# Modulation units that hold whole columns, placed later in the first mixer's load order, and the S5 matrices loaded from SyncE's queue

## The chip, the core and the metric

The kernel runs on one core of a Trainium2 chip. The metric is the device time of one execution in microseconds. All times below are of the kernel before the change.

## What is computed

The reference is two blocks over one sequence of 256 tokens, 1024 wide. Only the first part of the first block and the S5 branch of the second touch the change.

```python
def first_block(x, c, ...):
    cond = jax.nn.silu(c)
    mod = cond @ ada_w + ada_b                      # 1024 -> 6144
    sh1, sc1, g1, sh2, sc2, g2 = jnp.split(mod, 6)
    h = rms_norm(x, norm1_g) * (1.0 + sc1) + sh1
    y = hybrid_mixer(h, w_in, w_out, ...)           # four groups: attention a, attention b, GLA, LRU
    x = x + g1 * y
    h = rms_norm(x, norm2_g) * (1.0 + sc2) + sh2
    x = x + g2 * moe(h, ...)                        # 32 experts, 4 of them per token
```

The second block has two layers. Each is a SwiGLU feed-forward, a mixer (an SSD branch and an S5 branch), and a second feed-forward. The S5 branch is a diagonal complex recurrence, computed in chunks with small matrices (`win`, `E`, `toep`, `G`).

## The kernel before

Activations lie with features on the partitions, 256 tokens along the free axis. Every large weight is cut on the host into units of 128 x 2048 numbers (1 MB). `enqueue` puts all units of the program in one list. `load` issues the DMAs of this list in its order on SyncE's queue (SP), one whenever a raw buffer is free: three `raw` buffers, and two more (`rawx`) in the first mixer. A unit of a product is split into two halves, each into a high part (ScalarE, `whi`) and a low part (VectorE or GpSimd, `wlo`), and goes through TensorE in three passes (`mm3`: high by high, high by low, low by high). When both halves are split, the raw buffer is dropped and the next load is issued. A unit with a `use` function of its own is not split: `use` runs the function and drops the buffer. The 24 modulation units of `ada_w` are of this kind.

The order of work on each engine is fixed when the program is built. A planner (`Clocks`) keeps a modelled clock for each engine and for the DMA. `stir`, `tick` and `pump`, called between pieces of matrix product, step threads (attention a and b, GLA, LRU, the S5 build) when the modelled clocks say that their inputs are there. On the chip each engine then runs its own list strictly in order. Numbers such as `self.room` are counts of buffers that the planner has given out: `ps` are the eight PSUM banks, `p4` the large pages.

The first mixer (`mixer1`). The list begins with eight modulation units and two of the eleven input weights; after that come two modulation units behind each input weight, and at the end the four output weights `wo1`. Modulation unit u of `adaw` is 128 rows (one k) by 2048 columns, so eight units are needed before the first 2048 columns of `mod` are complete: `ada_unit` adds them up in one PSUM bank, which is held from unit 0 to unit 23, in four matmuls of 512 columns, each to its own 32 columns of TensorE's array. After each eighth unit `ada_turn` copies the bank to SBUF, transposes it and adds the bias. `use_up(7)` stands ahead of the products: it makes sure that shift and scale (`mod[:, :16]`) are complete. A loop over k then forms the normalised input `xn[k]`, and from k = 3 on multiplies with the first two input weights, cqk and cv, and the GLA gate. The other nine input weights follow in the order of `WIN`: cr, aq, ak, av, dx, dg, bq, bk, bv. A thread starts as soon as the products that it needs are there. Then `wo1` follows in the order of `YORD`: LRU, attention b, attention a, GLA; a group waits for its thread. The experts' weights are loaded into pages that the first mixer has used.

In the second block `ffn` consumes a unit for every 48 matmuls of 256 columns. While the first feed-forward of layer 0 and the second of layer 0 run, the thread `s5_build` loads the matrices of the next S5 branch, which were parked in DRAM during the experts: for each of two halves eight DMAs of 256 KB (`LT` from `ld`, `BT` from `s5_bt`, both read with a broadcast), a complex product of six operations (`cmul`, on GpSimd or VectorE) that makes `win`, and later four DMAs of 512 KB (`E`), sixteen of 64 KB (`toep`) and four of 512 KB (`G`). That is 40 DMAs and 9 MB in a layer. All are issued by GpSimd; the waits `GAP` between them (4 to 8 us) are of the planner's clock and place them in GpSimd's list, and are no waits on the chip.

Of the kernel before, what the change touches and what calls it, by code (L numbers as in the profile page):

```python
# [15 lines left out]
P = 128  # L16
# [179 lines left out]
class Core:  # L196
# [3 lines left out]
    stepping = GIVE = False  # L200
    KEEP = ("raw", "whi", "wlo", "ident", "causal", "ones_d", "ones_g", "eps", "one", "one32", "junk", "id16", "s5_r4", "vecs")
# [154 lines left out]
    def pump(self):  # L356

        c = self.nc
        while self.sl < self.sh and c.written(self.halves[self.sl][0]) <= max(c.tensor.clock, min(self.v.clock, self.q.clock)) + self.SOON:
            self.split_low()  # L360
        while self.sh <= min(self.most, 2 * self.last - 1) and self.arrived(self.order[self.sh // 2], c.scalar) and self.free(c.scalar):
            self.split_high()
        for u in sorted(self.uses):
            if not self.arrived(u, c.tensor):
                break
            self.use(u)
# [252 lines left out]
class Block2(Core):  # L619
# [406 lines left out]
    def s5_build(self, l, res):  # L1026
# [8 lines left out]
        for hf in range(2):  # L1035
            yield from self.need(p4=7)
            LT = self.p4([P, H, 64]), self.p4([P, H, 64])
            BT = self.p4([P, H, 64]), self.p4([P, H, 64])
            for g in range(2):
                rows = slice(g * 64, g * 64 + 64)  # L1040
                for ri in range(2):
                    self.lab = "s5b"
                    nc.gpsimd.dma_start(LT[ri][rows], dram_ap(ld, ((ri * 2 + g) * 4 * NP + hf * H) * 64, [[NP * 64, 4], [0, 16], [1, H * 64]]))
                    nc.gpsimd.dma_start(BT[ri][rows], dram_ap(a["s5_bt"], (((l * 2 + ri) * 2 + g) * 16 * NP + hf * H) * 64,
                                                            [[0, 4], [NP * 64, 16], [1, H * 64]]))
# [11 lines left out]
        for hf in range(2):  # L1057
            for ri in range(2):
                self.lab = "s5b"
                nc.gpsimd.dma_start(E[hf][ri].rearrange("p h m -> p (h m)"), made["ed"][hf, :, ri * 1024:ri * 1024 + 1024])  # L1060
# [4 lines left out]
        for hf in range(2):  # L1065
            for g in range(2):
                for j in range(4):
                    self.lab = "s5b"
                    r0 = g * 64 + j * 16
                    nc.gpsimd.dma_start(toep[hf][r0:r0 + 16], dram_ap(kd, hf * H * 32 * 112 + g * 16 * 112 + (3 - j) * 16,  # L1070
# [4 lines left out]
        for hf in range(2):  # L1075
            for ri in range(2):
                self.lab = "s5b"
                nc.gpsimd.dma_start(G[hf][ri].rearrange("p h k c -> p (h k c)"), made["gd"][hf, :, ri * 1024:ri * 1024 + 1024])
# [601 lines left out]
class Kernel(Block2):  # L1680
    NE, B1, NP42, NP22, NP12, NPAIR = 32, 2.0, 9, 8, 10, 4
    MIX = dict(EARLY=0.2, SOON=-0.5, LEAN=2.0, GIVE=True)
    WAT = 0, 3
    S3 = 0
# [7 lines left out]
    def block1_units(self):  # L1692
# [59 lines left out]
    def ada_load(self):  # L1752
# [3 lines left out]
        self.mod = self.t([P, 48], "mod")  # L1756

    def ada_unit(self, u, raw, n):

        nc = self.nc  # L1760
        g, k = divmod(u, KD)
        if not u:
            self.adaps = self.bank()
        lab, self.lab = self.lab, "ada"
        for i in range(4):
            nc.tensor.matmul(self.adaps[i * 32:i * 32 + 32], self.cond[:, k], raw[:, i * 512:i * 512 + 512], start=k == 0, stop=k == KD - 1,
                             skip_group_check=True, tile_position=(0, i * 32))
        if k == KD - 1:
            rows = self.t([P, 512], "adarow")
            nc.scalar.copy(rows, self.adaps)  # L1770
            if g == 2:
                self.give(ps=1)
            if g:
                self.defer(lambda: self.ada_turn(g, rows))
            else:
                for _ in self.ada_turn(g, rows):
                    pass
        self.lab = lab

    def ada_turn(self, g, rows):  # L1780

        nc = self.nc
        yield from self.need(ps=1)
        self.lab = "ada"
        ps = self.psum()
        for j in range(4):
            nc.tensor.transpose(ps[:, j * P:(j + 1) * P], rows[:, j * P:(j + 1) * P], self.ident)
        yield
        at = lambda t: t[:, g * 16:g * 16 + 16].rearrange("p (i j) -> p i j", j=4)
        self.v.tensor_tensor(at(self.mod), ps.rearrange("p (j i r) -> p i j r", j=4, r=32)[:, :, :, 0], at(self.vec("adab")), op=ALU.add)  # L1790
        self.give(ps=1)
# [479 lines left out]
    def mixer1(self, x):  # L2271
# [101 lines left out]
        self.use_up(self.keys.index(("ada", 23)))  # L2373
        for g in self.YORD:
# [8 lines left out]
            if last:  # L2383
                self.settle()
# [561 lines left out]
def host_block1(d, vecs, off):  # L2946
# [10 lines left out]
    out["adaw"] = c(f("ada_w").reshape(8, P, 3, 2048).transpose(2, 0, 1, 3).reshape(24, P, 2048))  # L2957
# [83 lines left out]
```

## Time and profile before

| what | us |
|---|---|
| median of three runs | 2945.7 (2922.97 to 2946.81) |
| the profiled execution, its own time | 2948.41 |
| its span, first to last instruction | 2946.7 |
| around the span | 1.7 |
| TensorE busy / DMA queue of SP, share of 16 engines | 2673.1 (91%) / 63.2% |

The span falls into stages: the first mixer to about 250 us, router and experts to about 1285, layer 0 of the second block to about 2142, and layer 1 to the end. PE is TensorE's matmuls, PEld its weight loads, DVE is VectorE, ACT is ScalarE, POOL is GpSimd; a name like `aq_raw<-adaw` is a DMA into a raw buffer from the tensor `adaw`. The prefix of a buffer's name is the label that the planner had when it was made, so modulation units have buffers of many names.

### The profile page before, as it was taken

The page shows a single profiled execution, that of the slowest core. Times are in us where ns is not written, and L with a number is a line of the kernel's source. Part 1 is how long each engine was busy: PE and PEld are TensorE (multiplying, and loading weights), DVE is VectorE, ACT ScalarE, POOL GpSimd, SP SyncE. Part 2 cuts the span into 40 slices and gives each one's busy share as a digit, 9 for nine tenths or more (in the row PEclk, how much of TensorE's full clock was granted, in tenths as well). Part 3 has the DMA queues.
Part 4 walks back from the last instruction along what each step waited for, and adds up shares of the span by engine and source line. Part 5 has one row for each costly group of instructions (what it writes and reads, how often), then busy time and mean ns, then how long its engine had stood idle before and what let it go on. Part 6 is the DMA issues. An engine that isn't in the chain of part 4 may idle for free.

```text
span 2946.7 us, 55258 instructions
## 1 busy us (share of the span) xinstructions
PE 2673.1 (91%) x22931; PEld 2049.9 (70%) x22931; DVE 1670.8 (57%) x2968; ACT 1009.0 (34%) x1474; POOL 423.4 (14%) x386
## 2 busy tenths in 40 slices
PE   6867898988898888988999999889999999998998
PEld 3656333332333333368999999889999999998998
DVE  3485324242333311056679787667575698977755
ACT  3273100001000000033454655434454455654544
POOL 2322100000000000034012131143010100221100
PEclk7788999999999999999999999999999999999999
DMA  8504999999999999977554544377455455553453
GB/s 333 214 31 146 420 420 405 415 420 420 420 415 416 420 419 419 418 243 206 203 184 167 189 172 170 137 160 241 172 189 180 149 180 189 186 190 125 159 185 115
DMA packets 145421, 754.62 MB, mean 256 GB/s; under 512 B 45760, under 2 KB 50320, under 8 KB 58640
## 3 DMA queue, kind: packets, MB, share of 16 engines
q1 hardware_dynamic: 127584, 710.42, 63.2%
q0 software_dynamic: 17440, 40.61, 5.3%
q8 instruction: 185, 3.03, 0.4%
q14 instruction: 68, 0.56, 0.1%
q10 hardware_dynamic: 144, 0.00, 0.0%
HBM read 735.98 MB, written 14.97 MB: 255 GB/s over the span
## 4 chain that ended last, share of the span: by engine, by line
PE 45%; DVE 7%; DMA 2%; ACT 2%; issue 1%; ACTq 0%; DVEq 0%
PE ffn_ps L172 21%; PE x_ps L172 4%; PE bb_ps L172 3%; PE z_ps L172 3%; PE glu_ps L172 3%; PE g_ps L172 3%; PE bnd_ps L172 2%; PE wo_ps L172 2%; DMA ffn_raw<-gu 1%; DVE ffn_wlo L172 1%; PE ssd_ps L172 1%; PE u_ps L172 1%; DVE ffn_p L172 1%; DVE x_p L172 1%; DVE bnd_p L172 1%
## 5 line engine op out<-in xcount | busy, mean ns | idle before, releaser
L172 PE MATMUL ffn_ps<-bnd_p,ffn_whi 128*128 128x256 f32 x2560 | 468.3, 285 | 0.5 <-ACT ffn_whi L172 0.5
L172 DVE TENSOR_TENSOR ffn_wlo<-ffn_raw,ffn_whi 128x1024 fp32r<-128x1024 f32 x232 | 305.5, 1322 | 189.9 <-ACT ffn_whi L172 189.8
L172 PEld LDWEIGHTS ffn_ps<-bnd_p,ffn_whi 128*128 128x128 f32 x2560 | 404.0, 194 | 0.9 <-ACT ffn_whi L172 0.9
L172 PE MATMUL ffn_ps<-bnd_p,ffn_wlo 128*128 128x256 f32 x1280 | 365.7, 286 | 17.5 <-DVE ffn_wlo L172 17.5
L172 ACT CAST ffn_whi<-ffn_raw 128x1024 fp32r<-128x1024 f32 x232 | 240.6, 1046 | 310.8 <-PE ffn_ps L172 242.1
L172 PE MATMUL down_ps<-up_place,tr_p 128*32 128x512 f32 (+1 forms) x2048 | 243.1, 612 | 81.1 <-DMA up_place<-edn 81.1
L172 PE MATMUL ffn_ps<-ffn_p,ffn_whi 128*128 128x256 f32 x1408 | 259.6, 286 | 11.3 <-ACT ffn_whi L172 11.3
L172 PEld LDWEIGHTS ffn_ps<-bnd_p,ffn_wlo 128*128 128x128 f32 x1280 | 248.5, 194 | 19.0 <-DVE ffn_wlo L172 19.0
L172 PE MATMUL up_ps<-down_place,prep_p 128*32 128x512 f32 (+1 forms) x1920 | 224.7, 596 | 21.0 <-DMA down_place<-eup 21.0
L172 PE MATMUL up_ps<-up_place,prep_p 128*32 128x512 f32 (+1 forms) x2048 | 230.5, 595 | 7.5 <-DMA up_place<-eup 7.0
L172 PEld LDWEIGHTS down_ps<-up_place,tr_p 128*32 128x32 f32 x2048 | 68.2, 112 | 243.0 <-issue 202.9
L172 PEld LDWEIGHTS ffn_ps<-ffn_p,ffn_whi 128*128 128x128 f32 x1408 | 223.3, 195 | 11.7 <-ACT ffn_whi L172 11.7
L172 DVE TENSOR_SCALAR glu_p<-up_ps 128x512 f32<-128x512 f32 x64 | 44.2, 691 | 311.2 <-PE up_ps L172 311.2
L172 PE MATMUL ffn_ps<-ffn_p,ffn_wlo 128*128 128x256 f32 x704 | 201.5, 286 | 1.1 <-DVE ffn_wlo L172 1.1
L172 PEld LDWEIGHTS up_ps<-up_place,prep_p 128*32 128x32 f32 x2048 | 61.8, 109 | 149.8 <-issue 129.8
L172 PEld LDWEIGHTS up_ps<-down_place,prep_p 128*32 128x32 f32 x1920 | 57.0, 109 | 130.7 <-issue 127.0
L172 DVE COPY scat_p<-down_ps 128x512 f32<-128x512 f32 x16 | 11.1, 692 | 240.4 <-PE down_ps L172 240.4
L172 PEld LDWEIGHTS ffn_ps<-ffn_p,ffn_wlo 128*128 128x128 f32 x704 | 137.1, 195 | 1.9 <-DVE ffn_wlo L172 1.9
L172 DVE TENSOR_TENSOR ffn_p<-ffn_p,ffn_p 128x256 f32<-128x256 f32 (+1 forms) x184 | 99.6, 547 | 41.6 <-ACT ffn_p L172 41.4
L172 ACT COPY prep_p<-prep_ps 128x512 f32<-128x512 f32 x16 | 9.4, 585 | 291.2 <-PE prep_ps L172 291.2
L172 ACT COPY tr_p<-tr_ps 128x512 f32<-128x512 f32 x32 | 18.7, 585 | 223.6 <-PE tr_ps L172 223.6
L172 PE MATMUL bb_ps<-ssd_p,ba_whi 128*128 128x256 f32 x416 | 84.2, 302 | 9.5 <-ACT ssd_p L172 6.1
(794 smaller groups left out, 5887.4 us busy)
## 6 DMA issues: line engine op xcount, KB each, us to landing
up_place<-eup SPq DMA_DIRECT2D x128, 1024.0 KB, 10.8
up_place<-edn SPq DMA_DIRECT2D x128, 1024.0 KB, 13.7
down_place<-eup SPq DMA_DIRECT2D x120, 1024.0 KB, 14.7
ffn_raw<-gu SPq DMA_DIRECT2D x75, 1024.0 KB, 4.9
ffn_raw<-dn SPq DMA_DIRECT2D x40, 1024.0 KB, 5.0
x_raw<-win SPq DMA_DIRECT2D x22, 1024.0 KB, 5.0
z_raw<-win SPq DMA_DIRECT2D x16, 1024.0 KB, 5.1
g_raw<-win SPq DMA_DIRECT2D x10, 1024.0 KB, 4.9
```

Source lines behind the costliest of these rows:

```text
L172: return f(out, *args, **kw)
```

## The change

Three things change. The modulation weights are cut by columns: unit u holds all eight k of 256 columns, so its eight matmuls complete these columns. For u below 8 they are column tile u of the shift and of the scale; for the others they are two neighbouring tiles. Each unit takes a PSUM bank of its own, and is copied, summed over the four column groups by two small matmuls with `four`, and added to its bias. At most two are under way (`room["ada"] = 2`). The loop over k asks for unit k alone, just ahead of `xn[k]`. In the list, two modulation units stand ahead of the first input weight and two ahead of the second; the other 16 follow one behind each input weight from av on (six) and behind the first two output weights (four and six). `pump` uses a modulation unit only when the modelled landing is 2.0 us ago and a bank is free, and the last ones are asked for only at the last output group. Third, all 40 DMAs of `s5_build` are issued on SP.

```diff
@@ Core.pump
         for u in sorted(self.uses):
-            if not self.arrived(u, c.tensor):
+            if u not in self.raws or c.written(self.raws[u][0]) > c.tensor.clock - self.ADAM or not self.has(dict(ps=1 + self.PSADA, ada=1)):
                 break
             self.use(u)
@@ s5_build (the same for BT, E, toep and G)
-                    nc.gpsimd.dma_start(LT[ri][rows], dram_ap(ld, ((ri * 2 + g) * 4 * NP + hf * H) * 64, [[NP * 64, 4], [0, 16], [1, H * 64]]))
+                    nc.sync.dma_start(LT[ri][rows], dram_ap(ld, ((ri * 2 + g) * 4 * NP + hf * H) * 64, [[NP * 64, 4], [0, 16], [1, H * 64]]))
@@ Kernel
+    ADA0, ADA1, ADAM = 5, (4, 6, 0, 0), 2.0
@@ block1_units
-        yield from ada[:8] + win[:2]
-        for j, u in enumerate(win[2:]):
+        yield from ada[:2] + win[:1] + ada[2:4] + win[1:2] + ada[4:8]
+        rest = iter(ada[8:])
+        for j, u in list(enumerate(win))[2:]:
             yield u
-            yield from ada[8 + 2 * j:10 + 2 * j]
-        for g in self.YORD:
+            if j >= self.ADA0:
+                yield next(rest)
+        for g, n in zip(self.YORD, self.ADA1):
             yield ("wo1", g), a["wo1"][g]
+            for _ in range(n):
+                yield next(rest)
@@ ada_unit (new body)
+        self.grab(ps=1, ada=1)
+        ps, w = self.psum(), raw.rearrange("p (k c) -> p k c", k=KD)
+        for k in range(KD):
+            i = k % 4
+            nc.tensor.matmul(ps[i * 32:i * 32 + 32, :T], self.cond[:, k], w[:, k], start=k < 4, stop=k >= 4, skip_group_check=True,
+                             tile_position=(0, i * 32))
+        if u < 8:
+            for _ in self.ada_turn(u, ps):
+                pass
+        else:
+            self.defer(lambda: self.ada_turn(u, ps), after=ps[:, :T])
@@ ada_turn (new body)
+        rows = self.t([P, T], "adarow", 2)
+        nc.scalar.copy(rows, ps[:, :T])
         yield
+        for j in range(2):
+            nc.tensor.matmul(ps[:, T + j * 32:T + j * 32 + 32], rows[:, j * P:(j + 1) * P], self.four, start=True, stop=True, skip_group_check=True)
+        yield
+        at = self.ada_at(u)
+        self.v.tensor_tensor(self.mod[:, at], ps[:, T:T + 64].rearrange("p (j r) -> p j r", r=32)[:, :, 0], self.vec("adab")[:, at], op=ALU.add)
+        self.give(ps=1, ada=1)
@@ mixer1
-        self.use_up(7)
...
-        v.scalar_tensor_tensor(A, self.mod[:, 8:16], 1.0, self.vec("norm1"), op0=ALU.add, op1=ALU.mult)
...
+            self.use_up(self.keys.index(("ada", k)))
+            v.scalar_tensor_tensor(A[:, k:k + 1], self.mod[:, 8 + k:9 + k], 1.0, self.vec("norm1")[:, k:k + 1], op0=ALU.add, op1=ALU.mult)
...
-        self.use_up(self.keys.index(("ada", 23)))
         for g in self.YORD:
...
             if last:
+                self.use_up(self.keys.index(("ada", 23)))
                 self.settle()
```

The host cuts `ada_w` to match.

## Rows read from the trace of the kernel before

**Rows 1.** Windows by stage: busy time by engine (count), granted clock, DMA share, GB/s.
```profile
100.00:150.00 50.00, 43.37 (x299) 36.67 (x298) 28.74 (x42) 15.71 (x24) 19.36 (x10) 0.81 0.43 150
350.00:1250.00 900.00, 792.76 (x6950) 298.54 (x6946) 267.15 (x787) 63.67 (x111) 17.84 (x28) 0.99 1.01 417
```

**Rows 2.** Waits, 50 to 270 us: total, times, longest.
```profile
PE mix_ps L172 <- DMA aq_raw<-adaw: 7.7, 2, 4.9
```

**Rows 3.** Timeline of PE in the first mixer: start, length, what.
```profile
60.33 0.80 PE L172 MATMUL cr_ps<-mix_p,mix_whi 128*128 128x256 f32 x2
...
179.06 0.28 PE L172 MATMUL bv_ps<-bk_whi,mix_p 128*128 128x256 f32 x1
...
249.28 0.28 PE L172 MATMUL bv_ps<-mix_p,wo_wlo 128*128 128x256 f32 x1
```

**Rows 4.** Windows of 5 us in the first mixer.
```profile
45.00:50.00 5.00, 5.00 (x46) 4.80 (x45) 1.23 (x1) 1.05 (x1) 0.00 (x0) 1.00 0.00 0
...
95.00:100.00 5.00, 5.00 (x24) 4.55 (x25) 1.36 (x3) 0.00 (x0) 0.00 (x0) 0.50 0.59 211
...
180.00:185.00 5.00, 0.00 (x0) 0.00 (x0) 4.90 (x8) 4.97 (x17) 4.82 (x3) 0.93 0.00 0
```

**Rows 5.** The chain of waits in order of time, around the four feed-forwards.
```profile
1299.76 22.93 PE ffn_ps L172 x191
1322.72 10.05 DVE ffn_wlo L172 x3
1335.49 18.64 DMA ffn_raw<-dn
...
1507.96 12.97 PE bnd_ps L172 x92
...
1916.27 4.89 PE bnd_ps L172 x39
1926.69 16.83 DMA ffn_raw<-gu
...
2142.07 4.88 PE bnd_ps L172 x39
...
2152.95 177.13 PE ffn_ps L172 x1476
...
2341.64 12.92 PE bnd_ps L172 x92
```

**Rows 6.** DMA view, 1280 to 1520 us: GpSimd's queue, packets, MB, share of 16 engines.
```profile
q0 software_dynamic: 6011, 9.44, 19.1%
```

**Rows 7.** Timeline of POOL: first and last of eight loads of one half, then its product.
```profile
1291.77 0.68 POOL L172 DMA_DIRECT2D s5b_p<-ld  x1
...
1296.02 0.60 POOL L172 DMA_DIRECT2D s5b_p<-s_bt  x1
...
1316.59 15.09 POOL L172 TENSOR_TENSOR s5b_p<-s5b_p,s5b_p 128x1024 f32<-128x1024 f32 x5 [4.84 <-DMA s5b_p<-s_bt]
```

**Rows 8.** Windows of 5 us in the first feed-forward of layer 0.
```profile
1300.00:1305.00 5.00, 5.00 (x44) 5.00 (x44) 4.64 (x8) 4.38 (x6) 0.00 (x0) 1.00 1.07 140
```

**Rows 9.** Timeline of all engines: the last of eight modulation units and what follows it.
```profile
26.76 1.94 PE L172 MATMUL mix_ps<-mix_raw,k_cond 128*32 128x512 f32 x8 [0.55 <-DMA mix_raw<-adaw]
...
28.76 0.58 ACT L172 COPY ada_adarow<-mix_ps 128x512 f32<-128x512 f32 x1 [16.79 <-PE mix_ps L172]
...
29.49 1.08 PE L172 MATMUL ada_ps<-k_ident,ada_adarow 128*128 128x128 f32 x4 [0.80 <-ACT ada_adarow L172]
30.62 0.17 DVE L172 TENSOR_TENSOR k_mod<-ada_ps,k_vecs 128x16 f32<-128x16 f32 x1 [14.73 <-PE ada_ps L172]
...
34.27 1.04 PE L172 MATMUL mix_ps<-mix_p,mix_whi 128*128 128x256 f32 x2 [3.70 <-ACT mix_p L172]
```

**Rows 10.** Groups of instructions, 0 to 330 us: busy us, mean ns.
```profile
L172 PE MATMUL gla_ps<-gla_p,gla_p 32*128 32x128 f32 x112 | 14.6, 329 | 1.7 <-DVE gla_p L172 1.7
```

**Rows 11.** The page's costliest groups: the low halves of the feed-forwards.
```profile
L172 DVE TENSOR_TENSOR ffn_wlo<-ffn_raw,ffn_whi 128x1024 fp32r<-128x1024 f32 x232 | 305.5, 1322 | 189.9 <-ACT ffn_whi L172 189.8
```

More of the change, by code (lines that the diff above doesn't have):

```diff
@@ L200 @@
     stepping = GIVE = False
+    ADAM, PSADA = 2.0, 0
     KEEP = ("raw", "whi", "wlo", "ident", "causal", "ones_d", "ones_g", "eps", "one", "one32", "junk", "id16", "s5_r4", "vecs")
@@ L1042, in s5_build @@
                     self.lab = "s5b"
-                    nc.gpsimd.dma_start(LT[ri][rows], dram_ap(ld, ((ri * 2 + g) * 4 * NP + hf * H) * 64, [[NP * 64, 4], [0, 16], [1, H * 64]]))
-                    nc.gpsimd.dma_start(BT[ri][rows], dram_ap(a["s5_bt"], (((l * 2 + ri) * 2 + g) * 16 * NP + hf * H) * 64,
+                    nc.sync.dma_start(LT[ri][rows], dram_ap(ld, ((ri * 2 + g) * 4 * NP + hf * H) * 64, [[NP * 64, 4], [0, 16], [1, H * 64]]))
+                    nc.sync.dma_start(BT[ri][rows], dram_ap(a["s5_bt"], (((l * 2 + ri) * 2 + g) * 16 * NP + hf * H) * 64,
                                                             [[0, 4], [NP * 64, 16], [1, H * 64]]))
@@ L1059, in s5_build @@
                 self.lab = "s5b"
-                nc.gpsimd.dma_start(E[hf][ri].rearrange("p h m -> p (h m)"), made["ed"][hf, :, ri * 1024:ri * 1024 + 1024])
+                nc.sync.dma_start(E[hf][ri].rearrange("p h m -> p (h m)"), made["ed"][hf, :, ri * 1024:ri * 1024 + 1024])
                 yield self.GAP[1]
@@ L1069, in s5_build @@
                     r0 = g * 64 + j * 16
-                    nc.gpsimd.dma_start(toep[hf][r0:r0 + 16], dram_ap(kd, hf * H * 32 * 112 + g * 16 * 112 + (3 - j) * 16,
+                    nc.sync.dma_start(toep[hf][r0:r0 + 16], dram_ap(kd, hf * H * 32 * 112 + g * 16 * 112 + (3 - j) * 16,
                                                                     [[112, 16], [32 * 112, H], [1, 64]]))
@@ L1077, in s5_build @@
                 self.lab = "s5b"
-                nc.gpsimd.dma_start(G[hf][ri].rearrange("p h k c -> p (h k c)"), made["gd"][hf, :, ri * 1024:ri * 1024 + 1024])
+                nc.sync.dma_start(G[hf][ri].rearrange("p h k c -> p (h k c)"), made["gd"][hf, :, ri * 1024:ri * 1024 + 1024])
                 yield self.GAP[1]
@@ L1756, in ada_load, with ada_at @@
         self.mod = self.t([P, 48], "mod")
+        self.room["ada"] = 2
+    def ada_at(self, u):
+        return slice(u, u + 9, 8) if u < 8 else slice(2 * u, 2 * u + 2)
     def ada_unit(self, u, raw, n):
         nc = self.nc
-        g, k = divmod(u, KD)
-        if not u:
-            self.adaps = self.bank()
+        self.grab(ps=1, ada=1)
         lab, self.lab = self.lab, "ada"
-        for i in range(4):
-            nc.tensor.matmul(self.adaps[i * 32:i * 32 + 32], self.cond[:, k], raw[:, i * 512:i * 512 + 512], start=k == 0, stop=k == KD - 1,
-                             skip_group_check=True, tile_position=(0, i * 32))
@@ L1768, in ada_unit @@
[L1768 to L1777, printed above, removed]
+        ps, w = self.psum(), raw.rearrange("p (k c) -> p k c", k=KD)
[3 more added lines that the diff above has]
+                             tile_position=(0, i * 32))
@@ L1778, in ada_unit, with ada_turn @@
+        if u < 8:
[3 more added lines that the diff above has]
+            self.defer(lambda: self.ada_turn(u, ps), after=ps[:, :T])
         self.lab = lab
-    def ada_turn(self, g, rows):
+    def ada_turn(self, u, ps):
         nc = self.nc
[L1783 to L1787, printed above, removed]
-        yield
-        at = lambda t: t[:, g * 16:g * 16 + 16].rearrange("p (i j) -> p i j", j=4)
-        self.v.tensor_tensor(at(self.mod), ps.rearrange("p (j i r) -> p i j r", j=4, r=32)[:, :, :, 0], at(self.vec("adab")), op=ALU.add)
-        self.give(ps=1)
+        rows = self.t([P, T], "adarow", 2)
+        nc.scalar.copy(rows, ps[:, :T])
+        yield
+        for j in range(2):
[4 more added lines that the diff above has]
+        self.give(ps=1, ada=1)
@@ L2956, in host_block1 @@
     out["c"] = c(np.asarray(d["c"]).reshape(8, P).T)
-    out["adaw"] = c(f("ada_w").reshape(8, P, 3, 2048).transpose(2, 0, 1, 3).reshape(24, P, 2048))
+    order = np.concatenate([np.arange(16).reshape(2, 8).T.reshape(-1), np.arange(16, 48)])
+    out["adaw"] = c(f("ada_w").reshape(8, P, 48, P)[:, :, order].reshape(8, P, 24, 2 * P).transpose(2, 1, 0, 3).reshape(24, P, 2048))
     addv("adab", f("ada_b"))
```

## The prediction

> **What bounds the kernel now.** I read the windows by stage first. From 350 to 1250 us the DMA share is 1.01 at 417 GB/s [rows 1]: the experts are bound by their weights, and their loads start only when the first mixer has left its pages. So what the first mixer saves moves everything behind it. The change touches two places: the first mixer and the two feed-forwards of layer 0 in which `s5_build` runs.
>
> In the first mixer neither the DMA nor an engine is full: from 100 to 150 us the DMA share is 0.43, VectorE is busy for 28.7 of 50 us, and TensorE's granted clock is 0.81 [rows 1]. The waits show why: two modulation units alone held TensorE for 7.7 us [rows 2], and behind such waits it runs at the lower of its two levels: 24 matmuls in 5 us at a granted clock of 0.50, against 46 in 5 us at 1.00 [rows 4]. TensorE meets the units in its fixed order, and the input weights wait behind them in the one list of loads. Nine of the eleven input products take from 60.33 to 179.34 us [rows 3], 119 us. Then the threads' tail begins: from 180 to 185 us TensorE does nothing, while VectorE is busy for 4.90 and ScalarE for 4.97 of 5 us [rows 4]. The last output matmul ends at 249.56 [rows 3].
>
> The chain of waits gives the second place. The first feed-forward of layer 1, which has no S5 loads beside it, goes from 2152.95 to the next boundary at 2341.64, 188.7 us; the same stretch of layer 0 goes from 1299.76 to 1507.96, 208.2 us, so 19.5 more. Counted from boundary to boundary, the second feed-forward of layer 0 takes 225.8 us (1916.27 to 2142.07) against 199.6 for layer 1's first (2142.07 to 2341.64), 26.2 more [rows 5]. The excess is **45.7 us**. Its chain holds DMA waits of 18.6 and 16.8 us, and three low halves that took 10.05 us [rows 5].
>
> **The change, part by part.**
>
> *The loop over k.* Before, eight units are awaited, and the loop runs through. Now each k has its own modulation on the path, and nothing is called inside the loop that could put other work between. For k = 4 to 7 a step is: eight matmuls, as long as one unit before (1.94 us at the lower clock, some 1.0 at the higher), a copy (0.58 for twice the columns, so at most that), two small matmuls (half of the four that took 1.08), the bias (0.17) [rows 9], the scale, three operations for `xn[k]`, and 15 matmuls: 1.6 or 3.1 us by the two rates [rows 4]. From copy to first product took 5.5 us before, with casts of weights between [rows 9]; without them I estimate 2.3. A step is then 4.9 to 7.4 us. The first products need k = 0 to 3 and the sixth load, where they needed the tenth. A load takes 2.5 us (1 MB at 417 GB/s [rows 1]); TensorE took the eighth as it landed, at 26.76 [rows 9], so the sixth, now the second input weight, lands two loads earlier, near 22 us. Its halves must be split; k = 3 is ready near 27, and its 60 matmuls end near 37. Four steps more: 57 to 66 us, where cr now starts. I take 62 against 60.3: **+2** (-3 to +6). The lost time of the serial steps eats what the earlier start wins.
>
> *The nine products.* Cr, aq and ak now follow without modulation units between, and each later unit is used 2 us after its modelled landing, so the 7.7 us and their like go, and with them most of the lower clock. TensorE's work to the last bv product: 432 matmuls at 46 in 5 us, 47 us; GLA's 14.6 [rows 10]; as much again, an estimate, for the rest of GLA and the start of attention a; eight modulation units at about 2 us, 16. That is 92, and with 2 for waits 94 against 119: **-25**. Bounds: 30 if everything packs, 0 if VectorE or ScalarE paces the stage as in the tail [rows 4]. I lean to the first end, since VectorE is at 57% in the row nearest to it [rows 1]. What is late next is the threads' VectorE work.
>
> *The tail.* Some eight units are left for it. Each costs ScalarE at most 0.58, VectorE 0.17 and TensorE 2.5 us [rows 9]. TensorE's part lies in its idle time; ScalarE's, at most 4.6 in sum, lies on a full engine. Against it, one PSUM bank is no longer held all through, and attention a gets its inputs as early, against bv, as before. I take **0** (-12 to +10). The tail is otherwise as long as it was, 70 us. The last units now load between output weights; if their cover failed, the last output group would wait for a load or two, inside the 10.
>
> *The 40 DMAs on SP.* GpSimd issued the eight loads of one half within 4.9 us [rows 7], whatever the planner had put between. They then shared the engines with the weights: 140 GB/s at a DMA share of 1.07 [rows 8], against 417 for weights alone. On SP they stand between weight loads, and SP waits at each of those for a raw buffer, one about every 5.7 us (33 units in 188.7 us). So a pair of 256 KB goes out for each weight. In the stage GpSimd's queue took 19.1% of 240 us, 46 us, for its 9.44 MB [rows 6]; 33 weights take 83; 129 of 189 us: it fits, but a pair (2.6 us at that queue's rate, 9.44 MB in 46 us; I bound it by twice that) and a weight (2.5) leave little during the two bursts. A weight may be 2 us late four times over, 8 us; three raw buffers and four split halves ahead cover that. So the DMA waits go. What stays is the product of the two halves: while GpSimd does its five operations of 15.09 us [rows 7], a low half takes 3.35 us (10.05 for three [rows 5]) instead of 1.32 [rows 11], 6.1 late in all. The full lead of halves hides a part; I take 3.4 for each of four bursts, 13.7 (0 to 24). 45.7 - 13.7 gives **-32** (-22 to -45.7). The 0.6 us of GpSimd for each issue lie off the path.
>
> On the queues themselves the row shows the loss beside two queues, and it cannot say whether the order or the mere bytes cause it. The Trainium skill speaks against this part (DMA: Bandwidth & Descriptors, section "Issuing engines are not separate DMA queues"): DMAs of every issuing engine run on the same 16 engines and interleave, so that another issuer saves only issue time. By that rule alone this part would be worth nothing, the second rival below. The same page (section "Queues, rings and completion order") says that each engine takes turns between queues; the row of 140 GB/s would agree.
>
> *Sum:* +2 - 25 + 0 - 32 = -55 on the profiled execution's 2948.4 (its span and 1.7 around it): **2893**. The median of the runs shown is 2.7 lower, well inside the range.
>
> **Rivals.**
>
> *Only the products gain (2925).* The parked loads' bytes and their patterns, not their order, hold the weights up, so the 45.7 us stay. For it: 46 us of share for 9.44 MB is poor in any queue. Against it: the same stage has idle DMA on either side of the bursts.
>
> *Only the loads gain (2921).* The stage of products turns into the tail's picture, VectorE and ScalarE full, and the loop runs at the lower clock: +5 - 32. For it: 4.90 and 4.97 of 5 us. Against it: 57% before.
>
> *Both at their good ends (2858).* -3, -30, -12 and -45.7.
>
> *SP is held up (2988), slower.* A parked load needs its large page free. If SP has to wait for one, all weights behind it wait as well, which on GpSimd's list they did not. It decides from a hold longer than the lead, three raw buffers at 5.7 us, 17 us. Held for twice that, once for `E` and once for `toep` in each layer, it costs 4 x 17 = 68 on top of the old excess, less 23 to 28 from the first mixer: +40. Against it: the first load went out without a wait, and the others right behind it [rows 7], so the pages are free.
>
> *The plan is laid anew and nothing comes of it (2945).* The planner prices a load alike in both queues and may put the threads worse.
>
> **How the numbers follow.** Forecast 0.43; only the products 0.15; only the loads 0.19; both good ends 0.12; SP held 0.07; nothing 0.04. A measurement of this kernel tells about 1%, 29 us, from no change: the lines are 2919 and 2975 about the profiled time. Faster: the forecast nearly whole (0.42), the good ends (0.12), and somewhat under half of the two halves (0.14): 0.68. Slower: most of SP held, 0.06. Within: 0.26. The range leaves out SP's case and some of the good end and of the cases at no change: 2850 to 2935.
>
> **What would show it.** Right, if cr starts at 57 to 66 us, TensorE is at the higher clock from there to bv, bv ends near 156 and the last output matmul near 227; if SP's list holds parked loads between weights, the two feed-forwards of layer 0 come to about 196 and 206 us, and no DMA wait over 10 us stands in their chain. The first step is wrong if cr starts past 70; the second if TensorE waits for VectorE or ScalarE between cr and bv; the last if low halves of over 3 us or waits for weights fill as much as before. A first mixer ending past 245 us, or SP waiting before a parked load, would make the prediction wrong.

## The result and the profile after

The changed kernel takes **2961.1 us** (median of 11 runs, 2956.4 to 2965.9) against 2945.7 of before beside it (11 runs, 2923.0 to 2958.1); the ratio is 1.0058 (95% interval 1.0040 to 1.0076). That is 0.6% slower, small but clear of the scatter, and 68 us above the forecast. The profiled execution took 2965.1 us, 16.7 more than the one of before. By the marks of the prediction:

| stretch of the profiled execution, us | before | after | difference | forecast |
|---|---|---|---|---|
| start to first cr product | 60.3 | 68.7 | +8.4 | +2 |
| cr to last bv product | 119.0 | 128.3 | +9.3 | -25 |
| last bv to last output product | 70.2 | 71.3 | +1.1 | 0 |
| from there to the first boundary in layer 0 | 1035.9 | 1041.4 | +5.4 | 0 |
| first feed-forward of layer 0, its products | 198.2 | 198.2 | 0 | } -32 |
| second of layer 0 and first of layer 1, products | 404.5 | 399.0 | -5.5 | } |

The rest, -2.0, lies in the other stages. The 1041.4 of the experts is 1036 to 1042 in the runs below that leave them alone.

TensorE's timeline of after, which answers to [rows 3]:

```profile
68.74 0.63 PE L172 MATMUL cr_ps<-mix_p,mix_whi 128*128 128x256 f32 x2
...
196.75 0.28 PE L172 MATMUL bv_ps<-bk_whi,mix_p 128*128 128x256 f32 x1
...
268.07 0.28 PE L172 MATMUL bv_ps<-mix_p,wo_wlo 128*128 128x256 f32 x1
```

One step of the loop over k in after (timeline of all engines, k = 4; PEld left out):

```profile
42.49 1.07 PE L172 MATMUL ada_ps<-mix_rawx,k_cond 128*32 128x256 f32 x16
...
43.69 0.37 ACT L172 COPY ada_adarow<-ada_ps 128x256 f32<-128x256 f32 x1 [7.91 <-PE ada_ps L172]
44.11 0.63 PE L172 MATMUL ada_ps<-k_four,ada_adarow 128*128 128x32 f32 x4 [0.55 <-ACT ada_adarow L172]
44.85 0.16 DVE L172 TENSOR_TENSOR k_mod<-ada_ps,k_vecs 128x2 f32<-128x2 f32 x1 [8.62 <-PE ada_ps L172]
...
45.90 1.04 PE L172 MATMUL mix_ps<-mix_p,mix_whi 128*128 128x256 f32 x2 [1.15 <-ACT mix_p L172]
...
49.40 0.85 PE L172 MATMUL ada_ps<-mix_rawx,k_cond 128*32 128x256 f32 x12
```

TensorE waits twice in a step, 0.55 us for ScalarE's copy and 1.15 us for the scaled `xn[k]`, with nothing to put between. The four steps start at 42.49, 49.40, 56.27 and 61.95, so 26 us in all, as estimated (4 times 4.9 to 7.4); but the first four products ended at 42.6 instead of the forecast 37. They needed the second input weight, and SP issued it only at 22.47:

```profile
15.90 2.35 DVE L172 TENSOR_TENSOR mix_wlo<-k_raw,mix_whi 128x1024 fp32r<-128x1024 f32 x2
...
20.47 1.94 PE L172 MATMUL ada_ps<-k_raw,k_cond 128*32 128x256 f32 x16
...
22.47 0.33 SPq L172 DMA_DIRECT2D mix_raw<-win  x1
```

Ahead of this load SP waits 12.3 us for the landing of the third modulation unit and then 6.2 us for TensorE: the weight was given that unit's raw buffer, which TensorE leaves at 22.41. The buffer of the first input weight was free from 18.25 on, when its low halves were made, and went to a modulation unit behind it in the list.

The stage of products, in windows from cr to bv: the row of all instructions, then that of the modulation units' tile alone (busy time by engine, granted clock, DMA share, GB/s).

```profile
68.70:197.00 128.30, 110.80 (x894) 91.96 (x892) 71.00 (x126) 54.21 (x100) 48.02 (x33) 0.80 0.54 199
68.70:197.00 128.30, 34.28 (x320) 19.68 (x320) 2.52 (x16) 5.94 (x16) 0.80 0.54 199
```

TensorE is busy for 110.8 of 128.3 us, 34.3 of them for 16 modulation units. From 100 to 150 us, where [rows 1] have a granted clock of 0.81, after has 0.60, and VectorE has 17.3 us of work where it had 28.7; the experts' row is as before:

```profile
100.00:150.00 50.00, 39.14 (x252) 30.03 (x253) 17.27 (x28) 11.30 (x20) 13.06 (x11) 0.60 0.47 160
...
350.00:1250.00 900.00, 793.78 (x6924) 297.28 (x6920) 270.94 (x800) 66.48 (x116) 18.95 (x30) 0.98 1.01 416
```

What these 50 us look like, in the timeline of all engines:

```profile
131.76 1.93 PE L172 MATMUL ada_ps<-dx_raw,k_cond 128*32 128x256 f32 x16 [3.31 <-DMA dx_raw<-adaw]
...
133.74 7.35 SPq L172 DMA_DIRECT2D dx_raw<-adaw  x2
133.80 0.37 ACT L172 COPY ada_adarow<-ada_ps 128x256 f32<-128x256 f32 x1 [6.50 <-PE ada_ps L172]
...
135.07 0.90 PE L172 MATMUL ada_ps<-k_four,ada_adarow 128*128 128x32 f32 x4
136.07 0.16 DVE L172 TENSOR_TENSOR k_mod<-ada_ps,k_vecs 128x2 f32<-128x2 f32 x1 [9.46 <-PE ada_ps L172]
136.15 0.68 DVE L172 TENSOR_TENSOR gla_p<-gla_ps,k_p 128x512 f32<-128x512 f32 x1
```

TensorE waits 3.31 us for a unit that SP could issue only late; ScalarE's copy and VectorE's bias stand in their lists behind it, and VectorE's GLA product, whose input had been ready since 128.4, starts 0.08 us behind a bias that waited 9.46. The waits of the stage, summed (total, times, longest), answer to [rows 2]:

```profile
PE ada_ps L172 <- DMA dx_raw<-adaw: 8.6, 3, 3.3
PE ada_ps L172 <- DMA bk_raw<-adaw: 3.4, 1, 3.4
...
DVE k_mod L172 <- PE ada_ps L172: 42.9, 13, 9.5
ACT ada_adarow L172 <- PE ada_ps L172: 38.2, 11, 6.6
```

The chain of waits in layer 0 and the like stretch of layer 1 ([rows 5]):

```profile
1324.42 11.41 PE ffn_ps L172 x95
...
1338.24 16.45 DMA ffn_raw<-gu
...
1359.82 14.90 DMA ffn_raw<-gu
...
1390.59 14.90 DMA ffn_raw<-gu
...
1409.06 15.72 DMA ffn_raw<-gu
1431.84 89.19 PE ffn_ps L172 x730
...
2169.06 177.13 PE ffn_ps L172 x1476
```

SP's list in after does hold the parked loads between the weights (timeline of SP):

```profile
1338.24 0.34 SPq L172 DMA_DIRECT2D ffn_raw<-gu  x1
1338.62 0.54 SPq L172 DMA_DIRECT2D s5b_p<-ld  x1
1339.20 0.54 SPq L172 DMA_DIRECT2D s5b_p<-s_bt  x1
1344.00 0.33 SPq L172 DMA_DIRECT2D ffn_raw<-gu  x1
```

And yet the weight issued at 1338.24, ahead of its pair, is the chain's wait of 16.45 us. The order came out as meant, and the wait stayed.

### The profile page after: what moved, and what is told of

It reads as the page before. It is cut to its first block, busy times and chain, and to the rows that moved or that the text cites. A ratio compares the mean times of both kernels' runs of the same rounds, so it can differ in the third digit from the quotient of the medians.

```text
span 2963.4 us, 55862 instructions
## 1 busy us (share of the span) xinstructions
PE 2701.3 (91%) x23207; PEld 2076.6 (70%) x23207; DVE 1659.5 (56%) x2992; ACT 1017.2 (34%) x1495; POOL 373.4 (13%) x310
## 4 chain that ended last, share of the span: by engine, by line
PE 44%; DVE 6%; DMA 4%; ACT 2%; issue 1%; POOL 0%; ACTq 0%; DVEq 0%; SPq 0%
PE ffn_ps L172 19%; PE x_ps L172 5%; DMA ffn_raw<-gu 4%; PE bb_ps L172 3%; PE z_ps L172 3%; PE g_ps L172 3%; PE glu_ps L172 3%; PE bnd_ps L172 2%; PE wo_ps L172 2%; PE ssd_ps L172 1%; DVE ffn_wlo L172 1%; DVE bnd_p L172 1%; PE u_ps L172 1%; PE s5o_ps L172 1%; DVE ssd_p L172 1%
## 5 line engine op out<-in xcount | busy, mean ns | idle before, releaser
L172 PEld LDWEIGHTS ffn_ps<-bnd_p,ffn_wlo 128*128 128x128 f32 x1280 | 248.3, 194 | 13.8 <-DVE ffn_wlo L172 13.8
L172 PEld LDWEIGHTS down_ps<-up_place,tr_p 128*32 128x32 f32 x2048 | 68.2, 112 | 244.2 <-issue 204.6
L172 DVE TENSOR_TENSOR ffn_p<-ffn_p,ffn_p 128x256 f32<-128x256 f32 (+1 forms) x184 | 85.3, 469 | 41.3 <-ACT ffn_p L172 41.0
L172 ACT COPY tr_p<-tr_ps 128x512 f32<-128x512 f32 x32 | 18.8, 586 | 226.5 <-PE tr_ps L172 226.5
```

Source lines behind the costliest of these rows:

```text
L172: return f(out, *args, **kw)
```

## The experiments

All marks in one table: start of cr, last bv product, end of the mixer, products of the first feed-forward of layer 0, and those of the second together with layer 1's first (TensorE's timeline). Base is the kernel after unless it says otherwise. Most times are single runs (the kernel before, beside them, took 2938.8 to 2954.4), so the marks are what to read. The marks scatter too: seven kernels have the first mixer of after unchanged (after, units_only, plain_src, lt_plain, bt_plain, no_cmul, no_parked), and it ended between 263.3 and 268.3; that of before ended at 249.6 and 252.3. So a difference of under 5 us between two mixers tells nothing.

| kernel | time | cr | bv | mixer | ffn 1 | ffn 2 + 3 |
|---|---|---|---|---|---|---|
| before | 2945.7 | 60.3 | 179.3 | 249.6 | 198.2 | 404.5 |
| after | 2961.1 | 68.7 | 197.0 | 268.3 | 198.2 | 399.0 |
| loads_only | 2941.8 | 61.0 | 181.0 | 252.3 | 199.0 | 398.7 |
| units_only | 2961.5 | 68.9 | 194.4 | 264.1 | 209.5 | 397.3 |
| no_late | 2913.1 | 68.5 | 151.8 | 219.7 | 197.9 | 399.4 |
| before_no_late | 2889.3 | 53.7 | 137.2 | 205.8 | 194.6 | 394.8 |
| units_ahead | 2948.7 | 62.0 | 189.8 | 252.2 | 198.9 | 399.0 |
| margin6 | 2943.1 | 63.6 | 186.1 | 248.7 | 197.5 | 401.1 |
| ahead_m6 | 2938.1 | 63.0 | 181.0 | 245.2 | 198.3 | 399.7 |
| ahead_m12 | 2941.2 | 62.2 | 177.7 | 246.4 | 197.5 | 401.2 |
| old_places | 2965.1 | 71.2 | 208.0 | 270.6 | | |
| no_turn | 2970.3 | 68.9 | 229.1 | 278.8 | | |
| thin_load | 2946.6 | 71.0 | 192.6 | 253.0 | | |
| plain_src | 2920.6 | 68.2 | | 263.3 | 178.7 | 381.5 |
| lt_plain | 2948.3 | 68.8 | | 268.2 | 190.9 | 391.7 |
| bt_plain | 2944.9 | 69.4 | | 265.0 | 192.1 | 388.8 |
| no_cmul | 2945.3 | 68.9 | | 264.7 | 193.6 | 394.8 |
| no_parked | 2952.0 | 69.0 | | 267.2 | 194.7 | 394.3 |
| best_a | 2925.7 | 62.2 | 182.6 | 247.3 | 190.8 | 390.5 |
| best_b | 2955.7 | 62.9 | | 247.7 | 191.8 | 391.0 |

### One part alone

`loads_only` is the kernel before with the DMAs of `s5_build` on `nc.sync`; `units_only` is after with them back on `nc.gpsimd`.

> The kernel before with only its 40 parked loads on SP; the modulation units are as before. Theory (the bytes and patterns of the parked loads hold the weights up, not their order): first mixer ends at 249 to 250 us as before, first feed-forward of layer 0 gains 0 to 3 us, the second 3 to 6, so 2938 (2932 to 2946), and DMA waits of 14 to 18 us stay in the chain. Rival (the order on SP is worth what was forecast, and the changed first mixer only hid it): 2905 to 2925, no DMA wait above 10 us.

> The kernel after with its 40 parked loads back on GpSimd. Theory: the first mixer ends near 268 us as in the kernel after, and the feed-forwards of layer 0 lose the 4 to 8 us that SP's order gave: 2965 to 2972, the slowest of the four. Rival (SP's order itself costs, the loss sits in both parts): 2950 to 2960, faster than after.

Measured: `loads_only` 2941.8, ratio 0.9998 (0.9977 to 1.0018); `units_only` 2961.5, ratio 1.0066 (1.0038 to 1.0094). So the loss is the first mixer's, and the other queue is worth nothing that the time can tell. Both expectations hold in the main; `units_only` came at 2961.5 instead of 2965 or more, and the mixer of `loads_only` ended at 252.3 instead of 249 to 250. In the stage the sign of a gain is not settled: from GpSimd's queue to SP's, 602.7 us (198.2 + 404.5) become 597.7, the 606.8 of `units_only` become 597.2 in after, but the 589.4 of `before_no_late` become 597.3 in `no_late`. These runs agree with the Trainium skill (DMA: Bandwidth & Descriptors, section "Issuing engines are not separate DMA queues"), by which another issuer saves only issue time.

### The first mixer without the later units

```diff
-            if j >= self.ADA0:
-                yield next(rest)
...
-            for _ in range(n):
-                yield next(rest)
...
-                self.use_up(self.keys.index(("ada", 23)))
```

> The kernel after without the 16 later modulation units (not loaded, not multiplied; gates and the second shift and scale are set to a constant 0.1, so the output is another). Theory (TensorE, and behind it the ordered lists of ScalarE and VectorE, wait for these units' loads): cr still starts at 68 to 69 us, the nine products run through, bv ends at 160 to 170 and the last output matmul near 232 to 240. Rival A (VectorE and ScalarE are paced by the threads' own work): bv ends past 185 and the mixer past 255 all the same. Rival B (the late start of cr is all of the loss): bv ends near 188.

> The kernel before without its 16 later modulation units (not loaded, not multiplied, gates and the second shift and scale a constant 0.1, so the output is another). It prices the old form as no_late does the new one (48.6 us). Theory (the new form, with sixteen round trips instead of two, is dearer): the mixer ends at 212 to 222 instead of 249.6, 28 to 37 for the sixteen. Rival (both forms cost the same, and the loop over k is all of the loss): 199 to 205.

Windows from cr to bv of `no_late`, and of `before_no_late`:

```profile
68.50:151.80 83.30, 71.94 (x557) 67.75 (x555) 71.97 (x115) 51.85 (x89) 41.89 (x25) 0.88 0.30 104
```

```profile
53.70:137.20 83.50, 71.37 (x557) 67.00 (x555) 72.03 (x115) 51.95 (x89) 41.83 (x25) 0.90 0.30 104
```

`no_late` went past its theory, which had bv at 160 to 170 and the mixer's end at 232 to 240. The two stages are the same, 83.3 and 83.5 us, and so are the tails, 67.9 and 68.7. Only the head differs: 68.5 against 53.7. The sixteen units cost 48.7 us in the new form (268.3 - 219.7) and 43.7 in the old (249.6 - 205.8). So of the +18.8 of the mixer 13.8 are there without these units (219.7 - 205.8): the head. The 5.0 that are left would be dearer units, but they lie within the scatter of the marks, so that a unit became dearer is not shown. My expectation of 212 to 222 for `before_no_late` fell; its rival, that the loop is nearly all of the loss, came within a microsecond of 205.8.

The rows also price the units: the stage grows by 45.0 us, of which 34.3 are TensorE's own time in them, 4.6 its other work that became longer (110.8 - 34.3 - 71.9, at a clock of 0.80 for 0.88), and 6.1 idle time (17.5 - 11.4).

### Head, margin, place

`units_ahead` puts `use_up` of unit 7 and the whole `A` ahead of the loop again; `margin6` and `ahead_m12` change `ADAM`; `ahead_m6` is both; `old_places` has two later units behind each input weight from cr on and none behind `wo1`.

```diff
+        self.use_up(self.keys.index(("ada", 7)))
         xn = self.fm(dt=F32R), self.fm(dt=F32R)
...
-    ADA0, ADA1, ADAM = 5, (4, 6, 0, 0), 2.0
+    ADA0, ADA1, ADAM = 5, (4, 6, 0, 0), 6.0
```

> The kernel after with all of the first eight units used ahead of the loop over k and shift and scale made whole there, as before; the list of loads and the later units stay as in after. Theory (a step of the loop with a unit inside costs 6 to 7 us of waiting in a row): the loop's products come in one piece, cr starts at 57 to 63 us instead of 68.7, and the mixer ends 6 to 10 us earlier than after, near 259 to 262. Rival (what sets cr is the landing of the first loads, or the later units swallow the start): cr at 66 to 70, or an end of the mixer at 266 to 270 all the same.

> The kernel after with 6.0 instead of 2.0 us between a unit's modelled landing and its use. Rival (the margin is too small for what loads really take): waits of TensorE for adaw go, the mixer ends at 248 to 258. Theory (raw buffers, not the margin, set when loads go out, and units held longer hold buffers longer): the waits move but do not go, 262 to 275.

> The kernel after with its 16 later modulation units where they stood before: two behind each input weight from cr on, none behind an output weight. Theory (between 105 and 155 us the units stand behind an output weight that keeps its raw buffer until the tail, so they come one at a time through what is left): waits for adaw loads of 2.5 to 3.3 us go, bv ends at 175 to 190 instead of 197, the mixer at 252 to 262 instead of 268. Rival A (sixteen round trips cost the same wherever they stand): 265 to 272. Rival B (as before the change, units ahead of input weights delay these): bv past 197.

> units_ahead and margin6 together: the first eight units ahead of the loop, and 6.0 us of margin for the later ones. With units_ahead the mixer ended at 252.2, with margin6 at 248.7, in after at 268.3. Theory (two causes, a late head and later units used before they land): they add in part, 238 to 247. Rival (both mend the same loss, that of the head): 247 to 254.

> ahead_m6 with a margin of 12.0 instead of 6.0. In ahead_m6 TensorE still waits 5.4 us for two modulation loads and 5.1 for copies on ScalarE, and the mixer ends at 245.2. If later landing than planned is still what is left: 238 to 244. Rival (the units' own work, and raw buffers held longer, are what is left): 245 to 253.

With the units ahead of the loop, cr starts 6.7 us and the mixer ends 16.1 us earlier; the stage of products is as long as in after (127.8 us), and what shortens is the time behind it, 62 us instead of 71. So the last bv product, by which I had reckoned, is not the mark that sets the end. Which thread does is not shown: GLA's last product moves from 231.3 to 200.8 us here, but in `old_places` it is at 206.6 and the mixer ends at 270.6. The mixer's end, 252.2, is earlier than the 259 to 262 of the expectation.

`margin6` went against my theory (the mixer at 262 or later) and to its rival: 248.7. Its head gains as well: its second input weight is given the buffer of the first, goes out at 18.09 us instead of 22.47, and the first four products end at 37.2 instead of 42.6. TensorE's waits for modulation loads in the stage fall only from 13.7 to 8.1 us. `ahead_m6` ends at 245.2, as if the two added in part, but the same mixer ended at 247.3 and 247.7 in `best_a` and `best_b`, inside the rival's 247 to 254; whether they add is open. In `ahead_m12` no wait for a modulation load is left in the stage, and the mixer still ends at 246.4, so lateness is no longer what holds it. `old_places` wins nothing back: TensorE's waits for modulation loads fall from 13.7 to 9.8 us, none over 2.2, yet bv ends at 208.0 and the mixer at 270.6, where both rivals had put them. My theory, that output weights hold the raw buffers and that this is what costs, falls with it.

### What in a unit costs

`no_turn` leaves out `ada_turn` for units from 8 on; `thin_load` moves 128 KB of a unit.

```diff
-            self.defer(lambda: self.ada_turn(u, ps), after=ps[:, :T])
+            self.give(ps=1, ada=1)
```

```diff
+            c = slice(0, 256 if self.keys[self.du][0] == "ada" and self.keys[self.du][1] >= 8 else 2048)
-            self.nc.sync.dma_start(raw, self.srcs[self.du])
+            self.nc.sync.dma_start(raw[:, c], self.srcs[self.du][:, c])
```

> The kernel after, the 16 later units loaded and multiplied as in after, but their copy on ScalarE, their two small matmuls and their bias on VectorE left out (gates and the second shift and scale are a constant 0.1, so the output is another). All 16 units together cost 48.6 us (268.3 against 219.7 without them). Theory (most of that is the round trip TensorE, ScalarE, TensorE, VectorE, in which ordered lists wait for a late load, with thread work behind it): the mixer ends at 235 to 248. Rival (TensorE's own wait for the loads and its work at the lower clock are all): 258 to 268.

> The kernel after; each of the 16 later modulation units loads only its first 256 of 2048 columns and multiplies these for every k, so its DMA moves 128 KB instead of 1 MB while its matmuls, copy and bias are all there (gates and the second shift and scale come out wrong). Theory (a third of the units' price is TensorE's wait for loads that land later than planned, 13.7 us between cr and bv, and two thirds their own work on TensorE): these waits go, the mixer ends at 250 to 258 instead of 268. Rival (only TensorE's work for the units counts): 262 to 268. Rival 2 (nearly all of the 48.6 us is the load): 220 to 235.

`no_turn` became slower, 278.8 us. The bank is given back at once, the plan comes out differently, and TensorE's waits for the units' loads grow from 13.7 to 18.7 us:

```profile
PE ada_ps L172 <- DMA dx_raw<-adaw: 11.4, 3, 5.2
...
PE ada_ps L172 <- DMA dg_rawx<-adaw: 5.0, 1, 5.0
```

The run can't price the round trip, since it moved the units as well; the theory that the round trip is most of the price has no support from it. `thin_load` ends at 253.0, inside the theory's range but not for its reason: with an eighth of the bytes TensorE still waits 6.4 and 4.6 us for two of these loads. They are late because SP issues them late, not because they are long: TensorE takes the two units at 98.13 and 150.20, so it was already waiting when SP issued them.

```profile
PE ada_ps L172 <- DMA ak_raw<-adaw: 6.4, 1, 6.4
PE ada_ps L172 <- DMA bq_raw<-adaw: 4.6, 1, 4.6
```

```profile
93.36 0.38 SPq L172 DMA_DIRECT2D ak_raw<-adaw  x1
...
147.61 0.33 SPq L172 DMA_DIRECT2D bq_raw<-adaw  x1
```

### The parked loads

`no_parked` sets the tiles with GpSimd and loads nothing; `no_cmul` has two products on VectorE for six operations; `plain_src` reads `LT` and `BT` from 64 plain rows, 8 KB apart, of matrices parked for `E` and `G`; `lt_plain` does so for `LT` alone, `bt_plain` for `BT` alone by a wider `s5_bt` from the host.

```diff
-  nc.sync.dma_start(LT[ri][rows], dram_ap(ld, ..., [[NP * 64, 4], [0, 16], [1, H * 64]]))
+  nc.sync.dma_start(LT[ri][rows].rearrange("p h m -> p (h m)"), made["ed"][hf, rows, ri * 1024:ri * 1024 + 1024])
-  nc.sync.dma_start(BT[ri][rows], dram_ap(a["s5_bt"], ..., [[0, 4], [NP * 64, 16], [1, H * 64]]))
+  nc.sync.dma_start(BT[ri][rows].rearrange("p h m -> p (h m)"), made["gd"][hf, rows, ri * 1024:ri * 1024 + 1024])
```

> The kernel after without its 40 parked loads in each layer; GpSimd sets the 18 tiles of a layer to a constant instead, the complex products stay, and the S5 branch gives other numbers. In after the two feed-forwards of layer 0 take 235.2 us (first boundary after the experts to the first mixer product) and 240.2 (boundary to the first feed-forward of layer 1), 475.4 in sum. Theory (their bytes hold the weights up): 435 to 450. Rival (the products on GpSimd beside VectorE, or the stage itself, make the excess): 462 to 475.

> The kernel after with the complex product of each half replaced by two products on VectorE (two operations instead of six, none on GpSimd; the S5 branch gives other numbers); all loads stay. As predicted, the product costs 13.7 us for four bursts: the sum of the two feed-forwards falls from 475 to 458 to 466. Rival (the low halves' lead hides it): 470 to 477.

> The kernel after with LT and BT read from plain rows of parked matrices of the same size instead of with a broadcast (the same bytes, 4 KB runs, but each source row is read once, not 16 or 4 times; the S5 branch gives other numbers). Theory (the broadcast, in which many descriptors read the same row, is what makes these loads slow): the sum of the two feed-forwards falls from 475 to 450 to 465. Rival (mere bytes beside the weights): 470 to 478.

> As plain_src, but only LT is read from plain rows (in after each of its source rows is read by 16 neighbouring partitions in a row); BT stays as in after, and the S5 branch gives other numbers. The two feed-forwards of layer 0 took 475.4 us in after and 438.9 in plain_src. Theory (many descriptors in a row on one 4 KB row of DRAM slow the whole queue): nearly all of the 36.5 us comes back, 438 to 448. Rival (each of the two broadcasts costs its half of the bytes): 453 to 462.

> The kernel after with s5_bt laid out four times on the host, so that BT is read from 64 plain rows instead of 16 rows read four times, 16 rows apart; the result is the reference's. Theory (what slows is reading the same row in direct succession, as LT does): 468 to 476 for the two feed-forwards, nothing gained. Rival (each broadcast costs its half): 453 to 462.

The expectations count from boundaries whose first row in the chain differs from run to run, so I compare the products' own lengths in the table: 597.2 us in sum in after, 560.2 in `plain_src`, 582.6 in `lt_plain`, 580.9 in `bt_plain`, 588.4 in `no_cmul`, 589.0 in `no_parked`. The chain of `plain_src` shows what is lost: layer 0's first feed-forward is one run of TensorE, of the length that layer 1's has.

```profile
1316.04 177.13 PE ffn_ps L172 x1476
...
2126.17 177.13 PE ffn_ps L172 x1476
```

The same bytes from the same queue in the same places cost nearly nothing when they are read from plain rows: 19.5 and 17.5 us come back, 37.0 of the 38.8 us by which the two feed-forwards of layer 0 in after (198.2 and 198.0) exceed 178.7 each. So neither bytes nor order held the weights up, but the pattern in which `LT` and `BT` are read. Each of the two has its part: `lt_plain` 7.3 + 7.3 us, `bt_plain` 6.1 + 10.2. My theory that `LT`, with sixteen reads of a row in succession, is nearly all of it fell; its rival, each its half, holds.

What in the pattern costs the time, the DMA share tells in stretches in which parked loads are nearly all that is under way. The rows are of after, of `plain_src`, and of `best_b` (below), in which `LT` is read with no row twice:

```profile
1349.80:1350.60 0.80, 0.80 (x9) 0.80 (x8) 0.80 (x2) 0.00 (x0) 0.00 (x0) 1.00 0.27 97
```

```profile
1378.40:1379.80 1.40, 1.40 (x14) 1.40 (x13) 0.75 (x2) 0.43 (x1) 0.00 (x0) 1.00 1.04 214
```

```profile
1388.20:1390.40 2.20, 0.72 (x6) 0.51 (x5) 2.20 (x4) 1.67 (x3) 0.00 (x0) 1.00 0.24 76
```

A share of a quarter is four of the 16 DMA engines; from plain rows all 16 work. The first stretch lies inside the chain's wait of 16.45 us: twelve engines have nothing left to do, while the weight issued at 1338.24 is not yet whole. All three patterns with a quarter begin with a count of four (`[NP * 64, 4], [0, 16]`, `[0, 4], [NP * 64, 16]`, and in `best_b` `[NP * 64, 4], [16 * NP * 64, 16]`), the plain ones with 64 rows; in `lt_plain`, where only `BT` is left so, and in `bt_plain`, where only `LT` is, stretches of the remaining loads have 0.25. So what the loads lack is engines, and reading a row twice is not needed for it. That the first count of the pattern sets the number of engines fits all of these loads, but no run changes that count alone. It is a reading of SP's queue: in before, with GpSimd issuing eight of these loads at once, the share is 1.07 at 140 GB/s [rows 8], and plain rows were not tried there.

`no_parked` gives back only 8.2 us, as its rival has it, but its chain tells why: no wait for a load is left in its feed-forwards of layer 0, and all that is lost in the first lies ahead of 1355.77, where GpSimd, with no loads to wait for, sets its tiles and does its products beside VectorE's low halves.

```profile
1318.73 8.38 DVE ffn_wlo L172 x3
...
1346.58 3.31 DVE ffn_wlo L172
1349.88 3.13 DVE ffn_p L172 x2
1353.02 2.71 DVE ffn_wlo L172
1355.77 158.42 PE ffn_ps L172 x1306
```

`no_cmul` gives 4.6 + 4.2 = 8.8 us where 13.7 were forecast. It is no clean price of the products on GpSimd, since in its chain VectorE, which now makes them, waits 22.2 and 15.3 us for parked loads. Once the weights are in time, the products cost next to nothing: `plain_src` keeps them and is left with 1.8 us of the 38.8.

### Put together

`best_a` is `ahead_m6` with `bt_plain`. `best_b` also writes `ld` sixteen times during the experts and reads `LT` from 64 different rows.

```diff
-        ld = self.scratch([2, 2, 4, NP, 64], "ld")
+        ld = self.scratch([16, 2, 2, 4, NP, 64], "ld")
...
-                    ... [[NP * 64, 4], [0, 16], [1, H * 64]]))
+                    ... [[NP * 64, 4], [16 * NP * 64, 16], [1, H * 64]]))
```

> ahead_m6 with bt_plain: units ahead of the loop, a margin of 6.0, and s5_bt laid out four times on the host so that BT needs no broadcast. Theory (the three causes are apart): the mixer ends near 245 us, the feed-forwards of layer 0 give 16 us back, so 2922 (2914 to 2931), faster than before by 0.5 to 1%. Rival (the weights' waits return with another place in the stage): 2934 to 2942.

> best_a, and the parked ld written sixteen times during the experts (32 DMAs of 64 KB a layer in runs of 256 bytes, where there were two), so that LT needs no broadcast either. Theory: the low halves' waits go as in plain_src and the feed-forwards give another 15 to 20 us, less what 4.2 MB more of writes cost beside the experts' weights (10 us at 417 GB/s, 20 at half of it): 2902 to 2925. Rival (the writes cost the experts more than the loads gain): 2925 to 2950.

`best_a` takes 2925.7 us, ratio 0.9941 (0.9922 to 0.9959): faster than both kernels, as expected. `best_b` takes 2955.7, ratio 1.0044 (1.0030 to 1.0059), slower than both its theory and its rival. From the mixer's end to the first boundary it needs 1069.5 us instead of 1041.6 (GpSimd has 60.4 us of work from 350 to 1250 us, before 17.8; 45.4 of it are the issues of 64 writes of `ld`), and the feed-forwards gain nothing over `best_a`, although no row is read twice any more. Reading a row again is therefore not what slows `LT`: with sixteen real copies its loads still keep only a quarter of the DMA engines busy (0.24, above).

## Why the prediction was wrong

**The loop over k (+2, came +8.4).** The step's own price held: 26 us for four steps. What failed is that the sixth load "lands two loads earlier, near 22 us". SP issued it only at 22.47, because it was given the raw buffer of the third modulation unit, which TensorE leaves at 22.41; I had let loads follow each other at 2.5 us. The first four products then ended 5.6 us late. In `margin6`, where this load goes out at 18.09, they end at 37.2 and cr starts at 63.6, against 37 and 62 forecast. Against a head without later units the new one is worse by 14.8 us (68.5 to 53.7); before, with the later units ahead of the input weights, cr started 6.6 later (60.3), which hid that much.

**The nine products (-25, came +9.3).** The sum of 94 us had 76 for TensorE's other work, and 76.5 were measured (110.8 - 34.3), though at a clock of 0.80. Two terms failed. "Eight modulation units at about 2 us, 16": all sixteen came into the stage, at 2.14 us each, 34.3 (+18.3). "2 for waits": 17.5 (+15.5). 94 + 18.3 + 15.5 is the 128 of the trace. That units are used 2 us after their modelled landing did not take the waits away, 13.7 us before loads against 12.8 before; and TensorE was at the higher clock without a break only up to 100 us; from 100 to 150 the granted clock is 0.60. It fell behind two windows of 5 us in which TensorE was idle for 0.5 and 0.7 us. Of the rival in which VectorE and ScalarE pace the stage nothing came: VectorE has 71 us of work in 128.

**The tail (0, came +1.1)** came out right for this kernel, but by luck: the eight units that it was reckoned with were not in it, and other placings moved it by some 20 us.

**The 40 DMAs on SP (-32, came -5.5).** The order came out as planned, and the failed step is that the order would make "the DMA waits go". In after the excess hung on the source pattern of `LT` and `BT`, which the change left as it was and which keeps four of 16 DMA engines busy on SP's queue (share 0.27, against 1.04 from plain rows); the rival of 2925 had named "bytes and their patterns". What the waits of before, on GpSimd's queue, came from is not shown. The term for GpSimd's product, 13.7, is put at 8.8 by `no_cmul`, which is no clean price. SP's own hold, the slower rival, did not occur.

## What to carry to other kernels

Before a transfer is moved to another queue, read the DMA share while it runs alone, and give it a plain source pattern once: here a share of a quarter gave it away, and the pattern was worth 37 us where the queue was worth between 10 gained and 8 lost. Work that goes onto an engine that is busy for 72 of 83 us of a stage costs about its whole length (34.3 of the 45.0 us here), and a wait in its ordered list can be paid again by the engines whose next instructions stand behind it. When a loop is cut into steps that can start earlier, follow the buffers as well as the data: the early start needs the load to be issued early.

## What the hardware showed unexpectedly

- 256 KB loads on SP whose source pattern begins with a count of four keep a quarter of the 16 DMA engines busy (share 0.24 to 0.27); from 64 plain rows the share is 1.04. Issued between weights, they stretch a 1 MB load from 6.2 us between issue and landing (the median in `plain_src`) to 14.9 to 17.0 us, where the chain waits for it.
- Two matmuls to 32 columns (four records) hold TensorE for 0.73 us (11.6 us for 64 records in the stage of products), half as long as the eight matmuls of 256 columns ahead of them (22.7 us by subtraction from 34.3 for 16 units, 1.4 each): few columns did not make these matmuls cheap.
- A low half beside a GpSimd operation took up to 3.4 us instead of 1.23 (chain of after, at 1375.76 and 1336.99).
